# The one expert with two row blocks: its first layer's second half into the other four PSUM banks, and the next expert's first layer ahead of its second layer

## The chip, the cores and the metric

The kernel runs on one core of a Trainium2 chip. The metric is the device time of one execution in microseconds, taken as the median of several runs. The engines named below are TensorE (PE, matmuls; PEld is its weight load), VectorE (DVE), ScalarE (ACT), GpSimd (POOL) and SyncE (SP), which issues the weight loads.

## What is computed

One layer of a diffusion backbone over 512 latent tokens of width 1024: a state-space mixer with a pooling mixer, then a mixture of 32 experts of which each token takes four. The change lies in the mixture alone:

```python
def run_block(args):                 # hb: rows of tokens that chose expert e
    toks, e = args
    hb = x_pad[toks] @ w1[e] + b1[e]               # 1024 -> 2048: first layer
    g_part = jnp.minimum(hb[..., ::2], SWIGLU_LIMIT)
    u_part = jnp.clip(hb[..., 1::2], -SWIGLU_LIMIT, SWIGLU_LIMIT)
    act = g_part * jax.nn.sigmoid(SWIGLU_ALPHA * g_part) * (u_part + 1)
    return act @ w2[e] + b2[e]                     # 1024 -> 1024: second layer
```

The result of a row is multiplied by its gate and added to the token's row of the output. All is float32. An expert's weights are 12 MB, so the 32 experts read 384 MB.

## The kernel before

**Places and blocks.** Experts are taken in 32 places, sorted by how many tokens chose them. A place has a fixed number of rows: 64 (odd places here), or 80 to 128. Place 16 alone has two blocks, of 128 rows and of 64 rows, since the expert with the most tokens stands there.

**Pieces.** Weights come in pieces of 1 MB: `load` (line 1081, SP's queue) fills one of 11 `raw` tiles, and `split` makes of it a high part `hi` (ACT, line 1093) and a remainder `lo` (DVE, line 1094) that TensorE multiplies apart. There are three pairs of `hi` and `lo`, taken in turn. So a piece is split when TensorE is through with the piece three before it, and a load is issued when the `lo` of the piece eleven before it is made. A first layer is 8 pieces and a second layer 4; in place 16 the first layer is 4 pieces for its left half of columns (h = 0) and 4 for its right half (h = 1).

**Products.** `prod` (line 1357) multiplies one 128-deep slab of a piece into banks of 512 columns. A block with more than 64 rows takes three products for each bank (`hi` by `xh`, `hi` by `xl`, `lo` by `xh`). A block of 64 rows holds its own high and low parts side by side as 128 rows and takes two; its rows 64 to 127 are then added to its rows 0 to 63 by `rest` (ACT copies them to `b2h`, line 1326 or 1329) and a matmul with `slt`, beside the matmul that adds the bias (line 1337; for larger blocks line 1339).

**Banks.** PSUM has eight banks of 512 columns. Tag A is two tiles of two banks each (`bank("B")`), tag S four tiles of one bank (`bank("C")` for second layers, `bank("T")` for transposes). A first layer of an ordinary place fills the four banks of A. In place 16 each half fills them too: one tile for the 128-row block, one for the 64-row block. So h = 1 writes the banks out of which h = 0 is read.

**Activations.** `swiglu` reads a tile's columns (ACT line 1366; DVE lines 1371 and 1372), 1024 at a time, that is 512 gates and 512 values. `transposed` turns activations and gathered rows by TensorE (lines 1129 and 1139), ACT and DVE then making their high and low parts (lines 1131, 1132, 1143, 1144). `finish` (lines 1380 and 1382) scales a second layer's result and POOL adds it to the output rows in memory.

**Order.** In an ordinary place the second layer `C` of the place before is multiplied behind the first layer of the place, so that it covers the activations' work. Around place 16 the order of weights is: 16 left half with the second layer of 15 in its middle, 16 right half, then at once both blocks' second layer of 16 (bank S for block 0, bank A for block 1), then the first layer of 17. Nothing of another place stands between the right half and the second layer of 16. Within this, a scheduler sets the order of each engine's instructions when the program is built.

Of the kernel before, what the change touches and what calls it, by code (L numbers as in the profile page):

```python
# [97 lines left out]
def mixer_and_moe(tc, a):  # L98
# [1025 lines left out]
    def transposed(src, m, pool, name, bufs, tbank):  # L1124
        if m == LT:
            both = pool.tile([P, KT, 2, LT], F32R, name=name + "h", tag=name + "h", bufs=bufs)
            tp = tbank()
            for k in range(KT):
                PE.transpose(tp[:, k * LT:(k + 1) * LT], src[0:LT, k * P:(k + 1) * P], ident[0:LT, 0:LT])  # L1129
            v = tp.rearrange("p (k t) -> p k t", k=KT)  # L1130
            SC.activation(both[:, :, 0, :], v, AF.Copy)
            newest_part[0] = VE.tensor_tensor(both[:, :, 1, :], v, both[:, :, 0, :].bitcast(F32), op=ALU.subtract)  # L1132
            return (both.rearrange("p k i t -> p k (i t)"),)
        hi = pool.tile([P, KT, P], F32R, name=name + "h", tag=name + "h", bufs=bufs)
        lo = pool.tile([P, KT, P], F32R, name=name + "l", tag=name + "l", bufs=bufs)
        for h in range(2):
            tp = tbank()
            for k in range(4):
                PE.transpose(tp[:, k * P:k * P + m], src[0:m, (h * 4 + k) * P:(h * 4 + k + 1) * P],
                             ident[0:m, 0:m])  # L1140
            o = hi[:, h * 4:(h + 1) * 4, 0:m]
            v = tp.rearrange("p (k t) -> p k t", k=4)[:, :, 0:m]
            SC.activation(o, v, AF.Copy)
            newest_part[0] = VE.tensor_tensor(lo[:, h * 4:(h + 1) * 4, 0:m], v, o.bitcast(F32), op=ALU.subtract)  # L1144
        return hi, lo
# [112 lines left out]
def moe(tc, a, c_, cst, psa, psb, phx, pc, pd, g2, b1h, b2h, msum, top4, tab, last, table_out, acc_scr, halfneg,  # L1258
# [49 lines left out]
    def selector(p):  # L1308
        if CAPS[p][-1] == LT:
            SC.activation(slt[0:LT, 0:2, :], selm[0][0:LT, p:p + 1].unsqueeze(2).broadcast_to([LT, 2, LT]), AF.Copy)  # L1310
            SC.activation(slt[LT:P, 2, :], selm[0][LT:P, p:p + 1].broadcast_to([LT, LT]), AF.Copy)
            if len(CAPS[p]) == 1:
                return True
# [9 lines left out]
    def rest(banks):  # L1323

        if len(banks) == 1:
# [5 lines left out]
    def bias1(t, m, sl, h):  # L1331
        q = slice(2 * E * h, 2 * E * (h + 1))
        for j, bk in enumerate(halves(t)):
# [26 lines left out]
    def swiglu(t, m, out, plus=0.0):  # L1360

        v = t[0:m, :].rearrange("p (n two) -> p n two", two=2)
        n = 512
        g = pm.tile([P, n], F32, name="sg", bufs=SGB)[0:m, :]
        u = pm.tile([P, n], F32, name="su", bufs=SUB)[0:m, :]
# [32 lines left out]
    def C(p, blocks, sl=None, hooks=()):  # L1398
        e = ids[p]
        bks = [[bank("C") for _ in range(2)] if i == 0 else halves(bank("B")) for i in range(len(blocks))]  # L1400
# [11 lines left out]
        for (act, m, gcol, icol), bk in zip(blocks, bks):  # L1412
            if m == LT:
                rest(bk)
# [164 lines left out]
    for p in range(E):  # L1579
        e = ids[p] = expert(p)  # L1580
        m = CAPS[p][0]
        if p != MID:
# [23 lines left out]
            def first_half(h):  # L1606
                bias1(two[h], m, sl, h)
# [13 lines left out]
            else:  # L1621
                for h in range(2):
                    first_half(h)
                if pend is not None:
                    end = C(*pend)
            aT = transposed(act, m, "a", 1)
            pend = (p, [(aT, m, gtp[0][:, p:p + 1], ixi[0][:, p:p + 1])], sl)
        else:
# [3 lines left out]
            for h in range(2):  # L1632
                two = [bank("B") for _ in range(2)]
                for kk in range(KT // 2):
                    hi, lo = split(load(w1_pair(e, kk, h)))
                    for i in range(2):
                        q = slice(i * FF, (i + 1) * FF)
                        for j in range(2):
                            prod(halves(two[j]), ms[j], xs[j], 2 * kk + i, hi[:, q], lo[:, q])
# [3 lines left out]
                    if h == 0 and kk == 2:  # L1643
                        end()
                if h == 0:
                    sl = selector(p)
                rest([two[1]])
                for i in range(2):
                    bias1(two[i], ms[i], sl, h)
                    swiglu(two[i], ms[i], acts[i][:, h * 512:(h + 1) * 512])  # L1650
            aT0 = transposed(acts[0], ms[0], "a", 1)
            aT1 = transposed(acts[1], ms[1], "x", 1, (pc, phx)[nx[0] % 2])
            C(p, [(aT0, ms[0], gtp[0][:, p:p + 1], ixi[0][:, p:p + 1]), (aT1, ms[1], gt2[0], ix2[0][:, 0:1])], sl)()
            pend = end = None
            nxt = next_x(p + 1)
# [55 lines left out]
    if m == LT:  # L1711
        rest(bk)
# [110 lines left out]
```

## Time and profile before

| | before |
|---|---|
| median of 3 runs | 1787.97 us (1785.37 to 1789.52) |
| the profiled execution | 1785.24 us, of which its span is 1783.4 us |
| PE, DVE, ACT, POOL busy | 1634.9, 1524.0, 1170.2, 594.1 us |
| loads and stores of all queues | 521.44 MB, mean 292 GB/s |

The span runs from the first to the last instruction of the profiled execution; the execution's own time holds about 2 us more. The mixture of experts fills the last two thirds of the span, from about 640 us on. Busy times are averages over stages with different limits, so the rows below look at the stage around place 16 by itself.

### The profile page before, as it was taken

The numbers are of one execution on the slowest core, as the hardware profiler recorded it, in microseconds if no ns is written. First come the engines' busy times: TensorE is split into PE (matmuls) and PEld (weight loads), VectorE is DVE, ScalarE is ACT, GpSimd is POOL, SyncE is SP. The second block draws the span as 40 slices with busy tenths as digits, with TensorE's granted clock in tenths as the row PEclk, the third lists the DMA queues.
The fourth block names the chain that finished last, engine by engine and source line by source line (L and its number), as shares of the span: only waits on it lengthen the run. The fifth ranks groups of instructions, "written<-read, shape, count | busy, mean of one in ns | idle before, by whom it ended". The sixth has DMA issues, their size and how long they took to land. (4 is left out here: it accounts for less than half of the span.)

```text
span 1783.4 us, 21256 instructions
## 1 busy us (share of the span) xinstructions
PE 1634.9 (92%) x7311; PEld 1199.5 (67%) x7311; DVE 1524.0 (85%) x1486; ACT 1170.2 (66%) x1207; POOL 594.1 (33%) x287
## 2 busy tenths in 40 slices
PE   6999889998899899999999999999999998999995
PEld 2777667776777777767767667676666666666663
DVE  7767888987876989999989999966899999999994
ACT  6445336556643567787777877755678777787773
POOL 1213456779210102152040541502053454313302
PEclk9999899999999999999999999998999999999998
DMA  9646453323468789999999999985899999999973
GB/s 353 196 132 212 148 159 100 108 78 112 174 233 332 285 333 356 375 392 380 376 375 391 357 382 392 356 309 197 335 381 383 381 369 363 386 387 366 387 262 103
DMA packets 138417, 521.44 MB, mean 292 GB/s; under 512 B 14798, under 2 KB 44942, under 8 KB 106560
## 3 DMA queue, kind: packets, MB, share of 16 engines
q1 hardware_dynamic: 125446, 490.39, 72.4%
q0 software_dynamic: 6736, 16.70, 4.0%
q10 hardware_dynamic: 6122, 12.94, 2.2%
q8 instruction: 59, 0.97, 0.2%
q14 instruction: 54, 0.44, 0.1%
HBM read 508.26 MB, written 18.37 MB: 295 GB/s over the span
## 5 line engine op out<-in xcount | busy, mean ns | idle before, releaser
L1094 DVE TENSOR_TENSOR lo<-raw,hi 128x2048 fp32r<-128x2048 f32 x398 | 896.5, 2283 | 87.3 <-ACT hi L1093 83.3
L1093 ACT ACTIVATE hi<-raw 128x2048 fp32r<-128x2048 f32 x398 | 752.1, 1915 | 177.8 <-PE A L1357 111.0
L1382 POOL DMA_INDIRECT acc_scr<-y,ixi x32 | 216.7, 6773 | 544.8 <-DVE y L1380 444.6
L1357 PE MATMUL A<-lo,xh 128*128 128x512 f32 (+3 forms) x1072 | 315.4, 411 | 30.7 <-DVE lo L1094 26.7
L1357 PE MATMUL A<-hi,xh 128*128 128x512 f32 (+3 forms) x1072 | 308.9, 404 | 11.9 <-ACT hi L1093 8.0
L1357 PEld LDWEIGHTS A<-lo,xh 128*128 128x128 f32 (+3 forms) x1072 | 188.7, 185 | 117.7 <-DVE lo L1094 68.6
L1357 PEld LDWEIGHTS A<-hi,xh 128*128 128x128 f32 (+3 forms) x1072 | 194.7, 185 | 70.0 <-ACT hi L1093 10.6
L1117 POOL DMA_INDIRECT xg<-h_scr,ixi x30 | 113.1, 3771 | 256.5 <-PE S L1129 174.7
L1357 PE MATMUL S<-lo,ah 128*128 128x512 f32 (+3 forms) x512 | 163.9, 401 | 15.3 <-DVE lo L1094 15.2
L1357 PE MATMUL S<-hi,ah 128*128 128x512 f32 (+3 forms) x512 | 162.4, 398 | 1.7 <-DVE ah L1132 1.7
L1357 PE MATMUL A<-hi,xl 128*128 128x512 f32 (+3 forms) x544 | 154.5, 397 | 0.0
L1357 PEld LDWEIGHTS S<-lo,ah 128*128 128x128 f32 (+3 forms) x512 | 89.2, 181 | 50.3 <-DVE lo L1094 25.5
L1357 PEld LDWEIGHTS A<-hi,xl 128*128 128x128 f32 (+3 forms) x544 | 95.0, 175 | 31.7
L1357 PEld LDWEIGHTS S<-hi,ah 128*128 128x128 f32 (+3 forms) x512 | 91.1, 181 | 30.3 <-issue 3.1
L228 ACT ACTIVATE hi<-raw 128x1024 fp32r<-128x1024 f32 (+1 forms) x73 | 76.0, 1045 | 39.0 <-PE A L355 10.8
L231 DVE TENSOR_TENSOR lo<-raw,hi 128x1024 fp32r<-128x1024 f32 (+1 forms) x59 | 77.1, 1312 | 18.2 <-ACT hi L228 17.4
L1357 PE MATMUL S<-hi,al 128*128 128x512 f32 (+3 forms) x272 | 85.3, 394 | 0.0
L630 ACT ACTIVATE row<-row,nb 128x128 f32<-128x128 f32 x192 | 59.5, 389 | 37.1 <-POOL row L626 37.1
L336 PE MATMUL A<-hx,hi 128*128 128x512 f32 x160 | 66.2, 413 | 4.0 <-DVE at L378 2.5
L338 PE MATMUL A<-hx,lo 128*128 128x512 f32 x160 | 66.8, 417 | 0.0
L337 PE MATMUL A<-hx,hi 128*128 128x512 f32 x160 | 65.9, 412 | 0.0
L378 DVE SCALAR_TENSOR_TENSOR at<-A,cw,at 128x510 f32<-128x510 f32 (+1 forms) x80 | 57.8, 740 | 7.2 <-ACT at L374 6.6
(464 smaller groups left out, 2454.1 us busy)
## 6 DMA issues: line engine op xcount, KB each, us to landing
raw<-in_w_dram SPq DMA_DIRECT2D x384, 1024.0 KB
raw<-in_w_in_dram SPq DMA_DIRECT2D x36, 512.0 KB
mraw<-in_w_mod_dram SPq DMA_DIRECT2D x32, 512.0 KB
raw<-in_w_out_dram SPq DMA_DIRECT2D x14, 1024.0 KB
row<-cs_scr ACTq DMA_DIRECT2D x32, 384.0 KB
raw<-in_w_mod_dram SPq DMA_DIRECT2D x16, 512.0 KB
raw<-in_w_in_dram SPq DMA_DIRECT2D x16, 384.0 KB
xt<-in_x_dram SPq DMA_DIRECT2D x4, 512.0 KB
```

Of the source, the lines that this page charges most:

```text
L228: SC.activation(hi, r, AF.Copy)
L231: e.tensor_tensor(lo, r, hi.bitcast(F32), op=ALU.subtract)
L336: PE.matmul(lat, lhsT=hi[:, k, :], rhs=row_of(hxh, k), start=(k == 0), stop=False)
L337: PE.matmul(lat, lhsT=hi[:, k, :], rhs=row_of(hxl, k), start=False, stop=False)
L338: newest[0] = PE.matmul(lat, lhsT=lo[:, k, :], rhs=row_of(hxh, k), start=False, stop=(k == KT - 1))
L378: VE.scalar_tensor_tensor(ac[:, u:v], src[:, u + o:v + o], cw[:, j, ct:ct + 1], ac[:, u:v], op0=ALU.mult, op1=ALU.add)
L630: SC.activation(row[:, h, :], row[:, h, :], AF.Exp, bias=nb[:, c, i:i + 1])
L1093: ia = SC.activation(hi, r, AF.Copy)
L1094: i = VE.tensor_tensor(lo, r, hi.bitcast(F32), op=ALU.subtract)
L1117: PO.indirect_dma_start(out=t[0:m, :], out_offset=None, in_=h2_scr, in_offset=bass.IndirectOffsetOnAxis(ap=col[0:m, :], axis=0), bounds_ch ...
L1357: PE.matmul(bk[0:n, :], lhsT=u[:, k, 0:n], rhs=v[:, j * 512:(j + 1) * 512], start=(k == 0 and i == 0), stop=((last or m == LT and k == KT ...
L1382: PO.indirect_dma_start(out=acc_scr, out_offset=bass.IndirectOffsetOnAxis(ap=icol[0:m, :], axis=0), in_=y[0:m, :], in_offset=None, bounds_ ...
```

## The change

The right half of place 16 (h = 1) is written to the four banks of tag S, the left half stays in A. `swiglu` takes a bank at a time there (256 gates and 256 values) in both halves. The rows of place 17 are gathered and transposed inside the left half of 16, into a tile of their own (tag `xl` of pool phx, which a 64-row place doesn't use). The second layer of 16 is no longer done at the end of place 16 but is handed on as in the other places, so it stands behind the first layer of place 17; both its blocks use bank S, and its result is finished at once in place 17. For that, the part of `slt` which the second layer's bias takes is written in `rest`, just ahead of use, and no longer in `selector`: one instruction of 64 by 128 becomes two of 64 by 64, in all 64-row blocks.

```diff
     def selector(p):
         if CAPS[p][-1] == LT:
-            SC.activation(slt[0:LT, 0:2, :], selm[0][0:LT, p:p + 1].unsqueeze(2).broadcast_to([LT, 2, LT]), AF.Copy)
+            SC.activation(slt[0:LT, 0, :], selm[0][0:LT, p:p + 1].broadcast_to([LT, LT]), AF.Copy)
...
-    def rest(banks):
-
+    def rest(banks, p=None):
+
+
+        if p is not None:
+            SC.activation(slt[0:LT, B2, :], selm[0][0:LT, p:p + 1].broadcast_to([LT, LT]), AF.Copy)
...
     def swiglu(t, m, out, plus=0.0):
...
-        n = 512
-        g = pm.tile([P, n], F32, name="sg", bufs=SGB)[0:m, :]
-        u = pm.tile([P, n], F32, name="su", bufs=SUB)[0:m, :]
+        n = t.shape[-1] // 2
+        g = pm.tile([P, 512], F32, name="sg", bufs=SGB)[0:m, 0:n]
+        u = pm.tile([P, 512], F32, name="su", bufs=SUB)[0:m, 0:n]
...
     def C(p, blocks, sl=None, hooks=()):
         e = ids[p]
-        bks = [[bank("C") for _ in range(2)] if i == 0 else halves(bank("B")) for i in range(len(blocks))]
+        bks = [[bank("C") for _ in range(2)] for _ in blocks]
...
                 if pend is not None:
                     end = C(*pend)
+            if p == MID + 1:
+
+                end()
+                end = None
             aT = transposed(act, m, "a", 1)
...
             for h in range(2):
-                two = [bank("B") for _ in range(2)]
+
+                two = [[bank("C") for _ in range(2)] if h else halves(bank("B")) for _ in range(2)]
...
                     if h == 0 and kk == 2:
                         end()
+                        end = None
+
+                        nxt = transposed_(gather_(xgs[(nx[0] + 1) % 2], ixi[0][:, p + 1:p + 2], LT), LT,
+                                          (pc, phx)[nx[0] % 2], "x", 1, lambda: bank("T"), "xl")
                 if h == 0:
                     sl = selector(p)
-                rest([two[1]])
+                rest(two[1])
                 for i in range(2):
                     bias1(two[i], ms[i], sl, h)
-                    swiglu(two[i], ms[i], acts[i][:, h * 512:(h + 1) * 512])
+                    for j, bk in enumerate(two[i]):
+                        q = h * 512 + j * 256
+                        swiglu(bk, ms[i], acts[i][:, q:q + 256])
             aT0 = transposed(acts[0], ms[0], "a", 1)
             aT1 = transposed(acts[1], ms[1], "x", 1, (pc, phx)[nx[0] % 2])
-            C(p, [(aT0, ms[0], gtp[0][:, p:p + 1], ixi[0][:, p:p + 1]), (aT1, ms[1], gt2[0], ix2[0][:, 0:1])], sl)()
-            pend = end = None
-            nxt = next_x(p + 1)
+            pend = (p, [(aT0, ms[0], gtp[0][:, p:p + 1], ixi[0][:, p:p + 1]), (aT1, ms[1], gt2[0], ix2[0][:, 0:1])], sl)
```

Built programs show what this does to the order on an engine. First TensorE between the two halves of place 16, before. A is the tag of the banks, `sel` and `slt` rows are biases, `hi`, `xh` and the like rows are products.

```order
L1357 MATMUL A<-lo,xh 128x512 x2
L1339 MATMUL A<-b1h,sel 128x512 x2
L1337 MATMUL A<-b1h,slt 64x512
L1337 MATMUL A<-b2h,slt 64x512
L1337 MATMUL A<-b1h,slt 64x512
L1337 MATMUL A<-b2h,slt 64x512
L1357 MATMUL A<-hi,xh 128x512 x2
```

The same place in the change:

```order
L1360 MATMUL S<-lo,xh 128x512 x2
L1360 MATMUL S<-hi,xh 128x512 x2
L1340 MATMUL A<-b1h,slt 64x512
L1340 MATMUL A<-b2h,slt 64x512
L1340 MATMUL A<-b1h,slt 64x512
L1340 MATMUL A<-b2h,slt 64x512
L1360 MATMUL S<-hi,xl 128x512 x2
```

The 64-row block's biases, which stood ahead of the right half, now stand 22 products into it, and the right half's products go to S.

Next TensorE at the end of the right half, before; the rows with `con` are transposes of the activations, and `ah` and `al` their parts in the second layer of 16.

```order
L1357 MATMUL A<-lo,xh 128x512 x2
L1339 MATMUL A<-b1h,sel 128x512 x2
L1337 MATMUL A<-b1h,slt 64x512
L1337 MATMUL A<-b2h,slt 64x512
L1337 MATMUL A<-b1h,slt 64x512
L1337 MATMUL A<-b2h,slt 64x512
L1139 MATMUL S<-con_76,act 128x128 x4
L1129 MATMUL S<-con_76,act_9343 128x64 x4
L1357 MATMUL S<-hi,ah 128x512 x2
```

The same place in the change, where the A rows are the first layer of place 17:

```order
L1342 MATMUL S<-b1h,sel 128x512 x2
L1360 MATMUL A<-hi,xh 128x512 x4
L1360 MATMUL A<-lo,xh 128x512 x4
L1360 MATMUL A<-hi,xh 128x512 x4
L1360 MATMUL A<-lo,xh 128x512 x4
L1360 MATMUL A<-hi,xh 128x512 x4
L1340 MATMUL S<-b1h,slt 64x512
L1340 MATMUL S<-b2h,slt 64x512
L1340 MATMUL S<-b1h,slt 64x512
L1340 MATMUL S<-b2h,slt 64x512
L1360 MATMUL A<-lo,xh 128x512 x4
L1139 MATMUL S<-con_76,act 128x128 x4
```

Where the biases, the activations and their transposes stood one behind another, 20 products of place 17 now stand ahead of the biases, and four more ahead of the first transpose. Last, VectorE in the change while the first layer of 17 is multiplied; `su` and `act` rows are the activation's two steps, `al` and `xl` low parts behind transposes, `lo` the splits of pieces.

```order
L1094 TENSOR_TENSOR lo<-raw,hi 128x2048
L1375 SCALAR_TENSOR_TENSOR act<-sg,su 128x256
L1094 TENSOR_TENSOR lo<-raw,hi 128x2048 x2
L1374 TENSOR_SCALAR su<-S 64x256
L1144 TENSOR_TENSOR al<-S,ah 128x512
L1094 TENSOR_TENSOR lo<-raw,hi 128x2048
L1144 TENSOR_TENSOR al<-S,ah 128x512
L1375 SCALAR_TENSOR_TENSOR act_9349<-sg,su 64x256
L1094 TENSOR_TENSOR lo<-raw,hi 128x2048 x2
```

The activations of 16 are taken between the splits of place 17's pieces, where before they stood alone.

## Rows read from the trace of the kernel before

**Rows 1.** Page part 1: engine, busy us, share of span, instructions.

```profile
PE 1634.9 (92%) x7311; PEld 1199.5 (67%) x7311; DVE 1524.0 (85%) x1486; ACT 1170.2 (66%) x1207; POOL 594.1 (33%) x287
```

**Rows 2.** Windows: stretch, length, busy by engine, PEclk, DMA share, GB/s.

```profile
1130.00:1180.00 50.00, 49.64 (x218) 36.86 (x216) 44.45 (x29) 34.45 (x26) 17.72 (x4) 1.00 1.02 384
...
1180.00:1270.00 90.00, 80.82 (x326) 57.92 (x326) 55.04 (x43) 48.12 (x41) 11.64 (x5) 0.91 0.65 236
...
1270.00:1690.00 420.00, 398.92 (x1767) 275.43 (x1768) 393.79 (x263) 327.29 (x245) 158.18 (x23) 0.99 0.99 377
```

**Rows 3.** Windows of 10 us within that stage, same columns.

```profile
1190.00:1200.00 10.00, 10.00 (x45) 8.17 (x44) 6.39 (x4) 6.20 (x4) 0.00 (x0) 1.00 0.25 86
1200.00:1210.00 10.00, 7.42 (x26) 4.50 (x25) 6.72 (x7) 4.97 (x6) 0.00 (x0) 0.71 0.86 341
1210.00:1220.00 10.00, 10.00 (x48) 7.68 (x48) 0.69 (x1) 1.00 (x2) 0.16 (x1) 0.95 0.00 0
...
1230.00:1240.00 10.00, 7.88 (x28) 4.97 (x27) 6.12 (x8) 6.09 (x8) 3.51 (x1) 0.91 0.97 333
1240.00:1250.00 10.00, 9.85 (x37) 7.11 (x37) 9.99 (x5) 10.00 (x6) 3.21 (x1) 0.92 0.90 277
```

**Rows 4.** Waits of SP's queue, 1040 to 1330 us: total, times, longest.

```profile
SPq L1081 <- DVE lo L1094: 241.1, 88, 19.2
```

**Rows 5.** Timeline of DVE: start, us, operation, [idle before <-releaser].

```profile
1183.73 2.29 DVE L1094 TENSOR_TENSOR lo<-raw,hi 128x2048 fp32r<-128x2048 f32 x1 [0.39 <-ACT hi L1093]
...
1194.20 6.88 DVE L1094 TENSOR_TENSOR lo<-raw,hi 128x2048 fp32r<-128x2048 f32 x3 [2.94 <-ACT hi L1093]
1203.41 2.29 DVE L1094 TENSOR_TENSOR lo<-raw,hi 128x2048 fp32r<-128x2048 f32 x1 [2.33 <-ACT hi L1093]
...
1223.13 6.69 DVE L1094 TENSOR_TENSOR lo<-raw,hi 128x2048 fp32r<-128x2048 f32 x3 [2.21 <-ACT hi L1093]
...
1240.01 17.71 DVE L1094 TENSOR_TENSOR lo<-raw,hi 128x2048 fp32r<-128x2048 f32 x8 [2.29 <-ACT hi L1093]
...
1268.73 6.69 DVE L1094 TENSOR_TENSOR lo<-raw,hi 128x2048 fp32r<-128x2048 f32 x3 [1.51 <-ACT hi L1093]
```

**Rows 6.** Timeline of PE, same columns.

```profile
1180.09 0.73 PE L1339 MATMUL A<-b1h,sel 64*128 64x512 f32 x2
1183.24 0.63 PE L1357 MATMUL A<-hi,xl 128*128 128x512 f32 x2
1183.71 0.63 PE L1357 MATMUL A<-lo,xh 128*128 128x512 f32 x2
...
1204.47 0.69 PE L1337 MATMUL A<-b1h,slt 128*64 128x512 f32 x1 [1.93 <-ACT b2h L1326]
...
1207.09 1.11 PE L1139 MATMUL S<-con,act 128*128 128x128 f32 x4 [0.65 <-DVE act L1372]
...
1254.21 0.45 PE L1337 MATMUL A<-b1h,slt 128*64 128x512 f32 x1 [1.84 <-ACT b2h L1326]
...
1257.06 0.69 PE L1337 MATMUL A<-b1h,slt 128*64 128x512 f32 x1 [1.72 <-ACT b2h L1326]
...
1269.90 0.71 PE L1129 MATMUL S<-con,xg 64*128 64x64 f32 x8
```

**Rows 7.** Groups by shape, 1153 to 1290 us: busy, mean ns, idle before.

```profile
L1094 DVE TENSOR_TENSOR lo<-raw,hi 128x2048 fp32r<-128x2048 f32 x35 | 78.7, 2287 | 15.5 <-ACT hi L1093 15.4
...
L1144 DVE TENSOR_TENSOR al<-S,ah 128x512 fp32r<-128x512 f32 x2 | 1.4, 692 | 3.6 <-ACT ah L1143 3.6
...
L1144 DVE TENSOR_TENSOR xl<-S,xh 128x448 fp32r<-128x448 f32 x2 | 1.2, 608 | 0.0
...
L1311 ACT ACTIVATE slt<-selm 64x64 fp32r<-64x64 f32 x2 | 0.5, 252 | 2.6 <-PE A L1337 2.6
```

**Rows 8.** Timeline of POOL: the gather of place 17's 64 rows.

```profile
1126.43 13.67 POOL L1117 DMA_INDIRECT xg<-h_scr,ixi  x1 [0.31 <-PE A L1357]
```

More of the change, by code (lines that the diff above doesn't have):

```diff
@@ L1122, in mixer_and_moe, with transposed @@
     newest_part = [None]
-    def transposed(src, m, pool, name, bufs, tbank):
+    def transposed(src, m, pool, name, bufs, tbank, tag=None):
         if m == LT:
-            both = pool.tile([P, KT, 2, LT], F32R, name=name + "h", tag=name + "h", bufs=bufs)
+            both = pool.tile([P, KT, 2, LT], F32R, name=name + "h", tag=tag or name + "h", bufs=bufs)
             tp = tbank()
@@ L1329, in rest, with bias1 @@
                 SC.activation(b2h[LT:P, j * 512:(j + 1) * 512], bk[LT:P, :], AF.Copy)
-    def bias1(t, m, sl, h):
+    def bias1(bks, m, sl, h):
         q = slice(2 * E * h, 2 * E * (h + 1))
-        for j, bk in enumerate(halves(t)):
+        for j, bk in enumerate(bks):
             js = slice(j * 512, (j + 1) * 512)
@@ L1413, in C @@
             if m == LT:
-                rest(bk)
+                rest(bk, p)
         def end():
@@ L1606, in first_half @@
             def first_half(h):
-                bias1(two[h], m, sl, h)
+                bias1(halves(two[h]), m, sl, h)
                 swiglu(two[h], m, act[:, h * 512:(h + 1) * 512])
@@ L1638, in moe @@
                         for j in range(2):
-                            prod(halves(two[j]), ms[j], xs[j], 2 * kk + i, hi[:, q], lo[:, q])
+                            prod(two[j], ms[j], xs[j], 2 * kk + i, hi[:, q], lo[:, q])
                     if h == 0 and kk == 1:
@@ L1711, in moe @@
     if m == LT:
-        rest(bk)
+        rest(bk, p)
     x = bias2(bk, m, sl)
```

## The prediction

> **What bounds the kernel now.** I read the page's busy table first: no engine is full, TensorE at 92% and VectorE at 85% come nearest [rows 1], so the limit must be sought by stage. Windows of the mixture come next. On either side of place 16 the DMA engines have no spare time: a share of 1.02 at 384 GB/s in the 50 us before, 0.99 at 377 GB/s in the 420 us behind [rows 2]. There the weight loads bound the kernel, at 1.049 MB / 0.38 MB per us = 2.76 us for a piece. From 1180 to 1270 us their share is 0.65, that is 0.35 x 90 = 31.5 us in which nothing was loaded [rows 2]. This is the kernel's visible loss in the mixture, and the change works in just this stage.
>
> Why the loads stop is seen in three views. SP's queue waits for one thing alone, the making of `lo` by DVE (88 waits, the longest 19.2 us) [rows 4]: a load goes out when the split eleven pieces back is done. DVE's splits have a hole from 1186.0 to 1194.2, since the right half of 16 has to go tile by tile, and one from 1205.7 to 1223.1, and few of them until 1240 [rows 5]; the loads' share is 0.25 in 1190 to 1200 and 0.00 in 1210 to 1220 [rows 3]. The splits in turn wait for ACT's `hi`, which waits for TensorE to free one of the three pairs. So in this stage TensorE's progress bounds the loads. It is a heavy place: 16 has 16 slabs of 10 products in its first layer and 8 of 10 in its second, and one product takes (1183.71 - 1183.24) / 2 = 0.235 us [rows 6]; a piece of two slabs and 20 products takes 4.7 us, against 2.76 us for its load. But TensorE also wastes time: it is busy 80.8 of 90 us, so idle 9.2, and the granted clock is 0.91 of full, 0.09 x 90 = 8.1 us more [rows 2]. Together 17.3 us. The waits are those of the tail of 16: 1.93 us for `b2h` and 0.65 us for the activations near 1205, 1.84 and 1.72 us at the end of place 17 [rows 6], and behind each pair of them the clock falls to its lower level of 1.2 GHz for a few microseconds (shares of 0.71, 0.91 and 0.92) [rows 3].
>
> **The change, part by part.** I count from TensorE's first bias of the left half, 1180.09, to the transposes at 1269.90 which in the program stand behind three slabs of place 18: 89.8 us before [rows 6]. The same work in the new order:
>
> 1. Bias of the 128-row block 0.73 us [rows 6], and the 64-row block's four biases, now inside the right half, 4 x 0.235 = 0.9. The right half follows at once, since the banks of S are free. 80 products: 18.8 us. One wait between the halves goes (the copy to `b2h` and the activations no longer stand ahead of it).
> 2. Bias in S, 0.7. Place 17's first layer, 64 products or 15.0 us on TensorE, but DVE paces it. Two of its eight pieces are split before the right half ends, since three pairs are in turn; six remain, 6 x 2.287 = 13.7 us [rows 7]. DVE also takes the activations of 16 there: four pieces of two operations, 256 wide. From 512 columns at 692 ns and 448 at 608 ns, a column costs 1.3 ns [rows 7], so 256 take about 692 - 256 x 1.3 = 0.36 us, and eight 2.9. Two low parts behind transposes take 1.4, two more (place 18's rows) 1.2. Sum 19.2 us, with a piece's latency 20. The transposes and the 64-row block's biases fit into TensorE's 5 us of slack there.
> 3. At the end of 17 the copy to `b2h` is still waited for, once, 1.84 us; its second wait of 1.72 is covered, since 16 products of the second layer of 16 now stand between. Eight biases: 1.9.
> 4. Second layer of 16: 80 products, 18.8 us, bias 0.7, last transposes 0.3. Then three slabs of place 18, 36 products, 8.5 us. Four banks of A are free by then, so they go at full pace.
> 5. Place 17's transposes, moved into the left half: 0.7 us, taken by 1180 us.
>
> Sum 0.7 + 0.9 + 18.8 + 0.7 + 20 + 1.8 + 1.9 + 18.8 + 1.0 + 8.5 + 0.7 = 73.8 us, against 89.8: 16.0 us less. That is near the 17.3 us that TensorE wastes now, as it should be. I take off one fall of the clock, of the smallest size seen, (0.09 + 0.08) x 10 = 1.7 us [rows 3], for the wait at the end of 17: 14.3 us.
>
> The loads must gain as much for it to count. They lose 31.5 us now. In the new order they still lose in the right half, 4 x (4.7 - 2.76) = 7.8 us, and in the second layer of 16. There TensorE takes block 0 for three pieces before it touches block 1, so no pair comes free for the 36 products of block 0, the eight biases, the wait and the first eight products of block 1, about 8.5 + 1.9 + 1.8 + 1.9 = 14 us; a few loads stand out at its start, so perhaps 9 us are lost. 31.5 - 16.8 = 14.7 us, in agreement. Behind 18 the two kernels are alike, and as the loads are full for 420 us there (0.99) [rows 2], what they gain should last to the end.
>
> Edits at no cost: place 17's gather runs at 1126.43 in the old program already, 13.67 us on POOL [rows 8], because the scheduler took it ahead, and its place in POOL's queue is the same; its rows are there 20 us before they are wanted. Were they late, TensorE would stand in the middle of the left half, at most for the gather's 13.67 us. The split of `selector` adds one instruction of 0.25 us [rows 7] in each 64-row place, 16 or so, 4 us in all on ACT, which is busy 66% [rows 1]; loads hide it, and without that cover it would cost 4 us. At the last place, 0.25 us may show. ACT's activations by halves add eight fixed costs at the most, likewise below 2 us, between its splits. The new waits on TensorE's queue are for `b2h` at the start of the right half and for the copies from S during 17; behind them stand products whose operands are ready, so what they hold up is counted above as slack of 5 us.
>
> TensorE's clock is the term I trust least. In the rows it falls after waits of about 2 us on a lightly fed TensorE, 3.4 us lost near 1205 ((0.29 + 0.05) x 10) [rows 3]. The Trainium skill (TensorE: Matmul & The Clock Gate, section "A second HAM failure mode: psum-queue depth-cycling") says that a TensorE which idles briefly and often between groups of products can swing between its two clock levels, and loses throughput although each product is fast. By that rule a first layer paced by DVE, as place 17's becomes, would swing, and the gain would be that of the first rival below, 7.5 us, not 14.3. The trace bears it out in place 17 before; in the 50 us from 1130 on, where most of place 15's first layer is multiplied at a like pace, it doesn't (granted clock 1.00) [rows 2].
>
> **Rivals.**
> - *The clock falls three times, as now.* Place 17 is fed by DVE with gaps, and two waits remain. For it: 1.72 and 1.84 us of wait did it at 17 before [rows 6]. Against it: 16 products now part the waits. Price: two more falls of 3.4 us, gain 14.3 - 6.8 = 7.5 us: by the sum below, 1779.
> - *The loss only moves.* The second layer of 16 stands behind 17 and holds all three pairs; if the pieces loaded by then are too few, places 18 to 20 wait for data, and the hole of 14 us comes back in full with the 7.8 us of the right half, and the catching up of 17 at DVE's pace is lost too (20 - 15 = 5 us): 31.5 - 14 - 7.8 - 5 = 4.7 us, and with one more fall 1.3: no difference, about 1786.
> - *Slower: the clock stays low.* If TensorE, once it has fallen at the start of 17, doesn't rise until the second layer of 16 is through, the 15.0 + 18.8 us of products take twice that, of which 5 are slack of 17: 28.8 us lost, 14.5 slower, 1802. It decides once more than 14.3 us of full-clock products run at the lower level. Against it: the fall near 1205 was over soon in 1210 to 1220 (0.95), on dense products [rows 3].
> - *All of the loss goes.* If the loads keep up (more of them outstanding, no wait at the second layer of 16), up to 24 us may be won; 1764.
>
> **How the numbers follow.** Chances: forecast 0.57 (gain 9 to 20 us), three falls 0.19, loss only moves 0.10, slower 0.08, more than forecast 0.06. The sum is made against the profiled execution, 1785.2 us, and gives 1785.2 - 14.3 = 1770.9; the median of the runs shown is 2.8 us higher, which gives 1773.7. I say 1772. About 0.2% (3.6 us) is what a measurement of this kernel can tell from no change. The range 1764 to 1784 holds the forecast, the three falls and all but the extreme of "all goes"; outside stand most of "only moves" and the slower case. Faster by more than that: 0.57 + 0.19 + 0.06 = 0.82; within it 0.10; slower 0.08.
>
> **What would show it.** In the profile after: TensorE's products to S begin within 1 us of the bias at the left half's end; no wait for `act` at 0.65 us and no wait of 1.93 for `b2h` at the end of the right half; place 17's first layer takes about 20 us with DVE nearly full; the loads' share shows a dip in the right half and one of about 9 us in the second layer of 16, and no window of 0.00; the transposes that stood at 1269.90 come near 1254 to 1256; the lower clock appears once between 1200 and 1245. It would be wrong if TensorE waits for VectorE in place 17 for more than 5 us, if the clock stays at its lower level through the second layer of 16, or if loads behind 1270 are below a share of 0.97, so that time won is lost again.

## The result and the profile after

| | before | after |
|---|---|---|
| median, four runs each | 1787.68 us (1785.37 to 1789.52) | 1768.12 us (1763.72 to 1769.41) |
| the profiled execution, its span | 1785.24, 1783.4 us | 1769.41, 1767.6 us |

The ratio is 0.9898, 95% interval 0.9883 to 0.9913: the change makes the kernel faster, by 19.6 us between the medians and by 18.2 us from the ratio. The two profiled executions are 15.8 us apart, for that of before is shorter than any of these four runs and that of after is the longest. Line numbers are those of each run's own kernel: `prod` is L1357 before and L1360 after.

The busy times of the page, against [rows 1], tell nearly nothing:

```profile
PE 1626.3 (92%) x7311; PEld 1197.6 (68%) x7311; DVE 1524.6 (86%) x1494; ACT 1170.6 (66%) x1229; POOL 551.7 (31%) x287
```

The stages do. Windows after, columns as in [rows 2]:

```profile
1130.00:1180.00 50.00, 49.71 (x225) 37.10 (x224) 44.43 (x29) 36.41 (x28) 18.66 (x4) 1.00 1.02 379
1180.00:1270.00 90.00, 89.01 (x402) 67.13 (x401) 72.31 (x59) 60.97 (x56) 20.77 (x5) 1.00 0.86 303
1270.00:1410.00 140.00, 132.62 (x590) 92.56 (x589) 130.36 (x89) 108.39 (x85) 36.01 (x8) 1.00 0.99 380
```

In the stage around place 16 TensorE is busy 89.0 of 90 us, against 80.8, its granted clock is 1.00, against 0.91, and the loads' share is 0.86, against 0.65 [rows 2]. Ahead of it the rows are alike. For what follows, the third of these windows in the kernel before:

```profile
1270.00:1410.00 140.00, 133.28 (x595) 92.98 (x596) 132.17 (x89) 110.67 (x84) 60.61 (x9) 1.00 0.98 375
```

Windows of 10 us after, which answer to [rows 3]:

```profile
1190.00:1200.00 10.00, 10.00 (x45) 8.09 (x44) 6.71 (x9) 4.10 (x3) 0.00 (x0) 1.00 0.69 238
1200.00:1210.00 10.00, 10.00 (x46) 7.44 (x45) 7.51 (x8) 8.05 (x8) 0.00 (x0) 1.00 0.67 245
1210.00:1220.00 10.00, 10.00 (x53) 7.91 (x52) 10.00 (x9) 9.93 (x11) 0.00 (x0) 1.00 0.95 348
1220.00:1230.00 10.00, 9.01 (x40) 6.48 (x39) 9.96 (x10) 6.66 (x9) 9.48 (x1) 1.00 0.91 334
1230.00:1240.00 10.00, 10.00 (x45) 7.87 (x45) 5.62 (x6) 5.72 (x4) 0.00 (x0) 1.00 0.60 206
1240.00:1250.00 10.00, 10.00 (x43) 7.32 (x42) 8.03 (x7) 6.31 (x6) 0.62 (x1) 1.00 0.94 335
```

No window from 1180 to 1270 us is empty of loads any more, and none has a lower clock. The shares of 0.69 and 0.67 are the right half of 16, the 0.60 is its second layer. TensorE's timeline after, against [rows 6]:

```profile
1181.92 0.73 PE L1342 MATMUL A<-b1h,sel 64*128 64x512 f32 x2
1182.58 0.73 PE L1360 MATMUL S<-hi,xh 128*128 128x512 f32 x2
...
1202.26 0.73 PE L1342 MATMUL S<-b1h,sel 64*128 64x512 f32 x2
1202.92 1.19 PE L1360 MATMUL A<-hi,xh 128*128 128x512 f32 x4
...
1220.79 1.20 PE L1360 MATMUL A<-lo,xh 128*128 128x512 f32 x4 [0.35 <-DVE lo L1094]
...
1222.63 0.45 PE L1340 MATMUL A<-b1h,slt 128*64 128x512 f32 x1 [0.64 <-ACT b2h L1329]
...
1223.62 0.40 PE L1360 MATMUL S<-hi,ah 128*128 128x512 f32 x1
...
1233.30 0.63 PE L1360 MATMUL S<-hi,xh 128*128 128x512 f32 x2
...
1253.93 0.66 PE L1129 MATMUL S<-con,xg 64*128 64x64 f32 x8
```

The right half starts in S 0.66 us behind the bias, the first layer of 17 starts 0.66 us behind the right half's bias, and the only waits of any size are 0.35 us for a `lo` and 0.64 us for `b2h`. From the bias to the transposes that stood at 1269.90 it is 1253.93 - 1181.92 = 72.0 us, against 89.8. The stretch starts 1.8 us later than before, for place 17's transposes stand ahead of it now and this execution was already 1.3 us behind at the gather (1127.72 against 1126.43 [rows 8]); it ends 1269.90 - 1253.93 = 16.0 us earlier. SP's longest wait for `lo` (1040 to 1330 us) falls from 19.2 [rows 4] to 9.4 us:

```profile
SPq L1081 <- DVE lo L1094: 214.9, 87, 9.4
```

### The profile page after: what moved, and what is told of

Same layout as the page of the kernel before. It is cut to its first block, busy times and chain, and to the rows that moved or that the text cites. A ratio compares the mean times of both kernels' runs of the same rounds, so it can differ in the third digit from the quotient of the medians.

```text
span 1767.6 us, 21305 instructions
## 1 busy us (share of the span) xinstructions
PE 1626.3 (92%) x7311; PEld 1197.6 (68%) x7311; DVE 1524.6 (86%) x1494; ACT 1170.6 (66%) x1229; POOL 551.7 (31%) x287
## 4 chain that ended last, share of the span: by engine, by line
PE 49%; DVE 17%; DMA 14%; issue 10%; ACT 4%; POOL 4%; SPq 0%; DVEq 0%; POOLq 0%; ACTq 0%
PE A L1360 21%; PE S L1360 12%; DVE lo L1094 8%; DMA raw<-in_w_dram 5%; DMA acc_scr<-y,ixi 3%; ACT hi L1093 2%; DMA mraw<-in_w_mod_dram 2%; PE A L736 1%; PE A L737 1%; PE A L740 1%; PE A L1340 1%; DVE ac L459 1%; PE A L353 1%; PE A L354 1%; DMA raw<-in_w_mod_dram 1%
## 5 line engine op out<-in xcount | busy, mean ns | idle before, releaser
L1360 PE MATMUL A<-lo,xh 128*128 128x512 f32 (+3 forms) x1024 | 297.1, 410 | 30.0 <-DVE lo L1094 25.9
L1385 POOL DMA_INDIRECT acc_scr<-y,ixi x32 | 161.2, 5038 | 505.6 <-DVE y L1383 383.9
L1360 PE MATMUL A<-hi,xh 128*128 128x512 f32 (+3 forms) x1024 | 290.4, 403 | 11.2 <-ACT hi L1093 8.6
L1360 PEld LDWEIGHTS A<-lo,xh 128*128 128x128 f32 (+3 forms) x1024 | 179.1, 184 | 114.1 <-DVE lo L1094 67.6
L1117 POOL DMA_INDIRECT xg<-h_scr,ixi x30 | 128.0, 4267 | 323.3 <-PE S L1129 157.3
L1360 PEld LDWEIGHTS A<-hi,xh 128*128 128x128 f32 (+3 forms) x1024 | 184.4, 184 | 65.4 <-ACT hi L1093 11.4
L1360 PE MATMUL S<-lo,ah 128*128 128x512 f32 (+3 forms) x512 | 164.2, 401 | 14.8 <-DVE lo L1094 14.7
L1360 PE MATMUL S<-hi,ah 128*128 128x512 f32 (+3 forms) x512 | 161.8, 396 | 1.6 <-DVE ah L1132 1.6
L1360 PE MATMUL A<-hi,xl 128*128 128x512 f32 (+3 forms) x528 | 147.6, 396 | 0.0
L1360 PEld LDWEIGHTS S<-lo,ah 128*128 128x128 f32 (+3 forms) x512 | 88.9, 180 | 48.4 <-DVE lo L1094 23.6
L1360 PEld LDWEIGHTS A<-hi,xl 128*128 128x128 f32 (+3 forms) x528 | 91.8, 174 | 30.9
L1360 PEld LDWEIGHTS S<-hi,ah 128*128 128x128 f32 (+3 forms) x512 | 91.0, 180 | 30.9 <-issue 3.9
L231 DVE TENSOR_TENSOR lo<-raw,hi 128x1024 fp32r<-128x1024 f32 (+1 forms) x59 | 77.0, 1310 | 19.6 <-ACT hi L228 18.6
L1360 PE MATMUL S<-hi,al 128*128 128x512 f32 (+3 forms) x272 | 85.3, 393 | 0.0
```

Of the source, the lines that this page charges most:

```text
L231: e.tensor_tensor(lo, r, hi.bitcast(F32), op=ALU.subtract)
L1117: PO.indirect_dma_start(out=t[0:m, :], out_offset=None, in_=h2_scr, in_offset=bass.IndirectOffsetOnAxis(ap=col[0:m, :], axis=0), bounds_ch ...
L1360: PE.matmul(bk[0:n, :], lhsT=u[:, k, 0:n], rhs=v[:, j * 512:(j + 1) * 512], start=(k == 0 and i == 0), stop=((last or m == LT and k == KT ...
L1385: PO.indirect_dma_start(out=acc_scr, out_offset=bass.IndirectOffsetOnAxis(ap=icol[0:m, :], axis=0), in_=y[0:m, :], in_offset=None, bounds_ ...
```

## Experiments

The table gives every run beside the kernel before on the same chip. "TensorE lost" is worked out for 1180 to 1270 us as in the prediction: 90 us less its busy time, and 90 us times what its clock lacks. "Loads lost" is the share that the DMA engines lacked there and in 1270 to 1410 us, times the lengths. "Less" is (1 - ratio) x 1787 us. Shares are rounded to hundredths, so that a loss is good to about 1 us. The ratio and "less" are from all executions of a run, the two columns of losses from its profiled one alone; that of e1_banks is its slowest, 1797.25 us.

| run | ratio to before (95%) | less, us | TensorE lost | loads lost |
|---|---|---|---|---|
| before | 1 | 0 | 9.2 + 8.1 = 17.3 | 31.5 + 2.8 = 34.3 |
| after | 0.9898 (0.9883 to 0.9913) | 18.2 | 1.0 + 0 = 1.0 | 12.6 + 1.4 = 14.0 |
| e1_banks | 0.9985 (0.9972 to 0.9998) | 2.7 | 8.7 + 8.1 = 16.8 | 24.3 + 7.0 = 31.3 |
| e2_order | 0.9971 (0.9957 to 0.9985) | 5.2 | 8.0 + 5.4 = 13.4 | 27.9 + 0 = 27.9 |
| e3_rows | 1.0032 (1.0022 to 1.0043) | -5.7 | 14.2 + 8.1 = 22.3 | 31.5 + 7.0 = 38.5 |
| e4_small | 1.0028 (1.0012 to 1.0043) | -5.0 | 13.8 + 9.9 = 23.7 | 31.5 + 7.0 = 38.5 |
| e5_fill | 0.9983 (0.9970 to 0.9996) | 3.0 | 8.0 + 0 = 8.0 | 28.8 + 2.8 = 31.6 |
| e6_rows_act | 1.0010 (0.9998 to 1.0023) | -1.8 | 12.5 + 7.2 = 19.7 | 31.5 + 4.2 = 35.7 |
| e7_order_act | 0.9954 (0.9937 to 0.9971) | 8.2 | 6.7 + 1.8 = 8.5 | 23.4 + 1.4 = 24.8 |
| e8_less | 0.9887 (0.9867 to 0.9906) | 20.2 | 1.1 + 0 = 1.1 | 8.1 + 4.2 = 12.3 |
| e9_b1first | 0.9933 (0.9913 to 0.9952) | 12.0 | 3.0 + 5.4 = 8.4 | 18.9 + 1.4 = 20.3 |
| e10_inter0 | 0.9935 (0.9919 to 0.9951) | 11.6 | 3.0 + 3.6 = 6.6 | 19.8 + 1.4 = 21.2 |
| e10_inter1 | 0.9918 (0.9901 to 0.9936) | 14.7 | 1.3 + 0 = 1.3 | 14.4 + 1.4 = 15.8 |

In all of these the loading that was lost less agrees with the time that was won, within 4 us and mostly within 2. TensorE's lost time says the same within about 3 us except where its work differs: e5_fill has 6.3 us of work more, e8_less 7.5 us less.

**The parts by themselves.** First the banks and the small edits alone, the second layer of 16 at once as before. From the changed kernel:

```diff
-            pend = (p, [(aT0, ...), (aT1, ...)], sl)
+            C(p, [(aT0, ...), (aT1, ...)], sl)()
+            pend = end = None
+            nxt = next_x(p + 1)
...
```

> The right half of place 16 in the banks of tag S and its activations bank by bank, but the second layer of 16 done at once as before, and place 17's rows gathered behind it. Theory (the time was lost in the waits of TensorE at the tails of 16 and 17 and in the clock that falls behind them, and the new order is what covers them): only the 1.2 us between the halves go, 1783 to 1787. Rival (the loads' hole while the right half goes tile by tile out of A was the loss, so the banks are what counts): 8 us less or more, 1780 or below.

Median 1783.78 us. The theory holds, the rival falls. The right half no longer waits, but the tails do (`b2h` 1.54 us and activations 0.83 us at the end of the right half, `b2h` 1.84 and 1.75 us at the end of 17), and the clock falls as before, so that the TensorE time lost in the stage stays at 16.8 us.

Then the order alone: second layer of 16 behind 17's first layer, both halves in A, activations 512 wide.

```diff
-                two = [[bank("C") for _ in range(2)] if h else halves(bank("B")) for _ in range(2)]
+                tt = [bank("B") for _ in range(2)]
+                two = [halves(t) for t in tt]
...
```

> The new order alone: both halves of place 16 in the banks of tag A with activations 512 wide, place 17's rows early and its first layer ahead of the second layer of 16. Theory: most of the gain, but place 17 waits until the right half's banks are read, 2 to 4 us with a fall of the clock, so 1770 to 1777. Rival (the banks are what counts): within 5 us of the kernel before, 1783 to 1788.

Median 1781.21 us: 4 us above the theory's bound. TensorE's timeline at the start of the right half, first in the kernel before:

```profile
1182.67 0.74 PE L1357 MATMUL A<-hi,xh 128*128 128x512 f32 x2 [0.20 <-DVE su L1371]
```

The same place in e2_order, and the end of its right half:

```profile
1188.55 1.22 PE L1360 MATMUL A<-hi,xh 128*128 128x512 f32 x2 [3.72 <-DVE su L1374]
...
1211.55 0.45 PE L1340 MATMUL A<-b1h,slt 128*64 128x512 f32 x1 [1.45 <-ACT b2h L1329]
```

The right half waits 3.72 us for the activations to free A, where it waited 0.20 us before, and the clock is lower behind it (0.92 and 0.91 in the two windows from 1180 to 1200 us). To see which edit brought that, the early rows of place 17 alone, put into the kernel before:

```diff
                     if h == 0 and kk == 2:
                         end()
+                        end = None
+                        nxt = transposed_(gather_(xgs[(nx[0] + 1) % 2], ixi[0][:, p + 1:p + 2], LT), LT,
+                                          (pc, phx)[nx[0] % 2], "x", 1, lambda: bank("T"), "xl")
...
-            nxt = next_x(p + 1)
```

> The kernel before with place 17's rows gathered and transposed inside the left half of place 16, nothing else. Theory: 0.7 us of transposes move out of the stage that TensorE bounds, so 0 to 1 us less, no difference that can be measured. Rival (the early rows let place 17 start earlier): 3 us or more.

Median 1791.15 us, slower by 0.32%, which neither expected. The start of its right half, from the timelines; ScalarE first:

```profile
1182.35 1.91 ACT L1093 ACTIVATE hi<-raw 128x2048 fp32r<-128x2048 f32 x1
1184.29 1.07 ACT L1366 ACTIVATE sg<-A 128x512 f32<-128x512 f32 x2
```

VectorE there:

```profile
1184.30 2.29 DVE L1094 TENSOR_TENSOR lo<-raw,hi 128x2048 fp32r<-128x2048 f32 x1 [2.76 <-ACT hi L1093]
1186.51 0.68 DVE L1371 TENSOR_SCALAR su<-A 128x512 f32<-128x512 f32 x1
```

TensorE, the first products of the right half:

```profile
1187.25 1.22 PE L1357 MATMUL A<-hi,xh 128*128 128x512 f32 x2 [3.72 <-DVE su L1371]
```

And ScalarE in the kernel before:

```profile
1181.30 0.60 ACT L1366 ACTIVATE sg<-A 128x512 f32<-128x512 f32 x1
1181.79 1.91 ACT L1093 ACTIVATE hi<-raw 128x2048 fp32r<-128x2048 f32 x1
```

Before, `sg` of the first tile stands ahead of the next piece's `hi`. With the early rows the built program has the `hi` (1.91 us) ahead of `sg` on ScalarE, and the `lo` (2.29 us) ahead of `su` on VectorE. The bank is freed by `su`, so the products behind it wait 3.72 us, and the granted clock is 0.73 in the window from 1180 to 1190 us. The Trainium skill (PSUM — Partial Sum Buffer, section "Engine vs sequencer instructions") says that ScalarE's and VectorE's queues are strictly first in, first out; the trace agrees, with `sg` at 1184.29 just behind a `hi` that the waiting products didn't need.

The small edits alone (one instruction for the selector into two, 256-wide activations) do the like:

```diff
...
-                    swiglu(two[i], ms[i], acts[i][:, h * 512:(h + 1) * 512])
+                    for j, bk in enumerate(halves(two[i])):
+                        q = h * 512 + j * 256
+                        swiglu(bk, ms[i], acts[i][:, q:q + 256])
...
```

> The kernel before with the split of the selector instruction in all 64-row places and the activations of place 16 by 256 columns, nothing else. Theory: hidden by loads, within 1 us of the kernel before. Rival (each of 16 instructions of 0.25 us on ACT counts): 4 us slower, 1791 to 1792.

Median 1791.74 us. The rival's time came, but the profile puts the loss elsewhere than it said. TensorE loses 6.4 us more than before in the stage around place 16 (23.7 against 17.3), which is more than the whole 5.0, and there is a wait of 3.20 us, for the second bank's `sg` stands behind a `hi` on ScalarE. The two edits weren't run apart. ScalarE's timeline, then TensorE's:

```profile
1180.72 0.39 ACT L1368 ACTIVATE sg<-A 128x256 f32<-128x256 f32 x1
1181.01 1.91 ACT L1093 ACTIVATE hi<-raw 128x2048 fp32r<-128x2048 f32 x1
1182.81 0.38 ACT L1368 ACTIVATE sg<-A 128x256 f32<-128x256 f32 x1
```

The products that wait for it:

```profile
1185.72 1.19 PE L1359 MATMUL A<-hi,xh 128*128 128x512 f32 x2 [3.20 <-DVE su L1373]
```

Two kernels then mend VectorE's order by a rule: the `lo` of the right half's third piece behind the left half's first activation. In e6 it is added to the early rows alone, in e7 to the order alone.

```diff
                     hi, lo = split(load(w1_pair(e, kk, h)))
+                    if h == 1 and kk == 2:
+                        after(newest_lo[0], first_act, "the activations go ahead")
...
```

> The early rows alone as in the kernel that was measured 4 us slower than before, with one more rule of order: VectorE's split of the third piece of the right half stands behind the first activation of the left half, not ahead of it. Theory (that kernel lost its time because VectorE split a piece ahead of the activation that frees bank A, TensorE standing 3.7 us at the start of the right half, with a fall of the clock): the wait returns to 0.2 us and the time to that of before, 1785 to 1788. Rival (the gather or the transposes of the early rows cost the time): 1790 to 1792 as without the rule.

> The new order alone, both halves in the banks of tag A, with the same rule of order for VectorE. Theory: the 3.7 us at the start of the right half and the fall of the clock behind it go, so 5 us less than without the rule, 1774 to 1778; what is left against the whole change are the waits between the right half and place 17. Rival (the new order alone is worth little, the banks as such are needed): 1780 to 1782 as without the rule.

Medians 1788.28 and 1777.99 us. e7's time is within its theory's range, e6's 0.3 us above it. Against e3 the ratio of e6 is lower clear of the noise, so it was in the main the order that the early rows cost, and neither the gather nor the transposes. The wait falls to 2.14 us in either, not to 0.2, since the rule holds VectorE's `lo` alone and ScalarE's `hi` still stands ahead of `sg`. Of e7:

```profile
1186.82 0.74 PE L1360 MATMUL A<-hi,xh 128*128 128x512 f32 x2 [2.14 <-DVE su L1374]
...
1208.68 0.45 PE L1340 MATMUL A<-b1h,slt 128*64 128x512 f32 x1 [1.92 <-ACT b2h L1329]
```

So the order has 1.6 us less of wait and 3.6 us less of lost clock, and e7's ratio is 3.0 us below e2's; the two intervals overlap, so the 3 us aren't clear of the noise.

**The clock by itself.** Products that nobody reads, 26 in all, fill the tails of 16 and 17 in the kernel before.

```diff
+    def fill(n, u, v):
+        t = bank("T")
+        for _ in range(n):
+            PE.matmul(t, lhsT=u[:, 0, 0:P], rhs=v[:, 0:512], start=True, stop=True)
...
+                if p == MID + 1:
+                    fill(8, x[0], lo)
...
+                else:
+                    fill(10, xs[1][0], lo)
```

> The kernel before with products that nothing reads (10 at the end of the right half of 16, 16 at the end of place 17, 0.235 us each) set where TensorE waits for the copies to b2h. Theory (the clock falls because TensorE waits there): the lower clock near 1205 and 1255 goes, 6.8 us of it at each place, so 3.4 us each are won, less 0.4 and 1.9 us by which the fillers outlast the waits: 3 to 5 us less, 1782 to 1785. Rival (the clock falls there for another reason, or costs nothing since loads bound the stage): the lower clock stays, and 0 to 2 us more, 1787 to 1790.

Its window over the stage:

```profile
1180.00:1270.00 90.00, 81.97 (x362) 59.95 (x361) 56.05 (x44) 46.53 (x40) 12.41 (x5) 1.00 0.68 247
```

The fillers as a group by shape: count, busy, mean ns, idle before.

```profile
L1425 PE MATMUL S<-lo,xh 128*128 128x512 f32 x26 | 6.3, 392 | 0.0
```

Median 1783.68 us: the theory's time holds, and its rival falls. The granted clock is 1.00 in the whole stage, against 0.91. It isn't one execution alone: over the whole span the clock was 0.975 to 0.978 in ten executions, against 0.966 to 0.976 in 19 of the kernel before. So the fillers hold the clock up. That a wait by itself brings it down isn't shown: waits of 2.08 us for the activations, of 1.72 us for `b2h`, and of 0.92 and 1.20 us in 17's first layer are left in this profile, and no fall stands behind any of them. The 8.1 us of clock come back less 6.3 us for the fillers; waits shrink by 1.2 us. That leaves 17.3 - 8.0 - 6.3 = 3.0 us, which is what was measured. The loads still lose 28.8 us in the stage: a clock held up by work that isn't wanted is worth little here.

**What bounds the changed kernel in the stage.** 32 of the 64-row block's products are left out of the right half and the second layer of 16, 7.5 us of TensorE: those of its rows with the weights' `lo`.

> The changed kernel with part of the computation left out: in the right half and the second layer of place 16 the 64-row block takes one product in place of two for each bank (32 products, 7.5 us of TensorE). Loads are the same. Theory (after the change the stage is bound by TensorE's products alone, loads waiting for them): 6 to 8 us less than the changed kernel, 1760 to 1762. Rival (loads or VectorE bound the stage now): within 2 us of the changed kernel, 1766 to 1769.

Its windows over the stage and behind it:

```profile
1180.00:1270.00 90.00, 88.89 (x394) 65.43 (x393) 77.11 (x62) 66.17 (x61) 17.28 (x5) 1.00 0.91 331
1270.00:1410.00 140.00, 129.82 (x576) 89.92 (x575) 127.35 (x87) 105.42 (x82) 62.58 (x8) 1.00 0.97 366
```

Median 1767.4 us: the same as the changed kernel. The theory falls and the rival's time holds: in the changed kernel TensorE's products in this stage aren't what sets the time. In the stage the loads lose 4.5 us less than after (0.91 against 0.86), but 2.8 us more in the 140 us behind it (0.97 against 0.99). Why they are lost there, and what sets the time instead, was not settled; from 1330 to 1370 us TensorE waits 5.4 us in all for `lo` in it, against 3.9 us after.

The dip of 0.60 in 1230 to 1240 us was taken up next. VectorE in that stretch of the changed kernel:

```profile
1236.83 4.49 DVE L1094 TENSOR_TENSOR lo<-raw,hi 128x2048 fp32r<-128x2048 f32 x2 [4.06 <-ACT hi L1093]
```

It idles 4.06 us for `hi`, that is for a free pair, as the prediction described for the second layer of 16. Two kernels let TensorE take both blocks piece by piece, by holding back the `lo` of the second layer's first piece (inter0) or second piece (inter1).

```diff
             hi, lo = split(load(w2_pair(e, kk)))
+            if p == MID and kk == 0:
+                after(newest_lo[0], part1, "both blocks go together")
```

> The changed kernel with one rule more in the second layer of place 16: VectorE's low part of its first piece stands behind block 1's transposed activations, so that TensorE takes both blocks piece by piece there and the three pairs come free one after another, not all behind 36 products of block 0. Theory (the loads' dip of 1230 to 1240, share 0.60, comes from the three held pairs, and loads that aren't lost there count to the end): 2 to 5 us below the changed kernel, 1763 to 1766, with a share above 0.8 in each 10 us of the second layer. Rival (as with the products left out, loads gained around place 16 are given back by place 21, since the stretch behind is bound by something else too): 1767 to 1770, the same as the changed kernel. Second rival (the split that waits stands ahead of place 17's work on VectorE's queue, and TensorE waits for it): 1772 to 1780, with a wait for the low part of 2 us or more near 1225.

> As the run with the rule at the first piece, but the rule at the second piece: block 0's first piece goes ahead, then both blocks together. It holds VectorE's queue less, and frees the first pair no earlier than the changed kernel. Theory (held pairs cost loads): 1 to 3 us below the changed kernel, 1765 to 1767. Rival (given back): 1767 to 1770. Second rival (a split that waits): 1770 to 1776.

Medians 1772.01 and 1769.45 us. The theory falls with both; in inter1 the first rival's time (given back) holds, and its interval overlaps that of the changed kernel. In inter1 the dip moves, from 1230 to 1240 into 1240 to 1250 us, and isn't gone:

```profile
1230.00:1240.00 10.00, 10.00 (x46) 8.12 (x44) 5.89 (x3) 3.89 (x3) 0.00 (x0) 1.00 0.82 285
1240.00:1250.00 10.00, 10.00 (x45) 6.70 (x44) 8.65 (x8) 7.58 (x7) 3.50 (x1) 1.00 0.67 223
```

From 1220 to 1260 us the loads lose 6.0 us in it and 5.9 us in the changed kernel: the order in which the pairs come free didn't change the sum. That fits an estimate: 80 products take 18.8 us and the layer's four loads 4 x 2.76 = 11.0, so about 7.8 us have to be lost in either order. In inter0 the second rival's time holds, though the wait is for `b2h` and not for the low part:

```profile
1226.64 0.69 PE L1340 MATMUL A<-b1h,slt 128*64 128x512 f32 x1 [2.61 <-ACT b2h L1329]
```

Last, the right half's tail with the 64-row block ahead of the 128-row block:

```diff
-                for i in range(2):
+                for i in ((1, 0) if h else (0, 1)):
```

> The changed kernel with the biases and activations of the right half taken for the 64-row block ahead of the 128-row block. Theory (nothing waits for the order of the two there, since place 17's first layer covers both): within 2 us of the changed kernel, 1766 to 1770. Rival (what comes first on ScalarE and VectorE moves a split, as in the runs where early rows alone cost 3 us): 1771 to 1775, with a wait of 2 us or more between 1202 and 1225.

TensorE at the end of 17's first layer in it:

```profile
1221.04 0.45 PE L1340 MATMUL A<-b1h,slt 128*64 128x512 f32 x1 [0.64 <-ACT b2h L1329]
...
1224.16 0.69 PE L1340 MATMUL A<-b1h,slt 128*64 128x512 f32 x1 [1.99 <-ACT b2h L1329]
```

Its windows of 10 us there:

```profile
1220.00:1230.00 10.00, 7.37 (x31) 4.57 (x30) 9.64 (x11) 8.90 (x12) 0.43 (x1) 0.68 1.00 381
1230.00:1240.00 10.00, 10.00 (x37) 8.05 (x37) 3.79 (x7) 2.59 (x3) 0.55 (x1) 0.81 0.52 166
```

Median 1773.23 us: the rival holds, with a wait of 1.99 us and a clock fall of (0.32 + 0.19) x 10 = 5.1 us behind it. The products of 16's second layer, which stand between the two groups of biases in the changed kernel, come behind both here. That is the first rival of the prediction in small: with a second wait at 17's end and one fall back, 18.2 - 12.0 = 6.2 us of the gain go, for the order of two blocks.

## Why the prediction was right

**What bounds the stage: right for the kernel before.** The 17.3 us that TensorE wasted were named as what there is to win; 1.0 is left of them, and the loads' loss fell from 31.5 to 12.6 us. Across the runs above, these two track the time. For the changed kernel it holds no longer: 7.5 us less of TensorE's work bought 2.0 us by the ratios, within the noise (e8_less).

**The sum: right in the whole, with terms off both ways.** Bias and right half with four biases took 1202.26 - 1181.92 = 20.3 us (20.4 forecast). 17's first layer took 19.1 us up to the wait for `b2h` (20). That wait was 0.64 us (1.84). The second layer of 16, three slabs of 18 and the last four biases took 1253.93 - 1223.62 = 30.3 us (28.3 + 0.9 = 29.2). With the 0.7 us of transposes that the prediction counts ahead of the stretch, 72.7 us stand against its 73.8, or against 75.5 with the clock's 1.7.

VectorE was at work without a gap from 1203.85 us to the end of 17's first layer, as said. But TensorE was busy 18.7 of 19.1 us there too:

```profile
1202.92:1221.99 19.07, 18.72 (x91) 14.40 (x90) 18.00 (x15) 18.52 (x20) 1.54 (x1) 1.00 0.85 311
```

64 products, four biases and the transposes of 16 and of the next rows leave little of the 5 us of slack that had been reckoned. Which of the two engines set the layer's length this run can't tell, so that 20 us came near is in part luck. The 256-wide operation is 0.42 us, not 0.36:

```profile
L1375 DVE SCALAR_TENSOR_TENSOR act<-sg,su 128x256 f32<-128x256 f32 x4 | 1.7, 423 | 0.1
```

**The clock: the term that failed.** One fall of 1.7 us was taken off the 16.0; there was none. With TensorE filled there, waits of 0.35 and 0.64 us left it at 1.00. The rows were misread as well. The prediction puts the shares of 0.91 and 0.92 [rows 3] behind the waits of 1.84 and 1.72 us at the end of 17, but those windows end at 1250 us and the waits at 1254 and 1257. The fall of 1.7 us stands inside 17's first layer, behind two shorter waits (products of 0.43 us in place of 0.235), in the kernel before:

```profile
1235.39 0.73 PE L1357 MATMUL A<-lo,xh 128*128 128x512 f32 x2 [0.92 <-DVE lo L1094]
1237.33 0.70 PE L1357 MATMUL A<-hi,xh 128*128 128x512 f32 x2 [1.20 <-DVE y L1380]
...
1238.40 1.06 PE L1357 MATMUL A<-hi,xh 128*128 128x512 f32 x2
```

The end of 17 has a fall of its own there, of (0.23 + 0.11) x 10 = 3.4 us:

```profile
1250.00:1260.00 10.00, 6.38 (x20) 3.65 (x19) 9.30 (x7) 6.30 (x7) 0.00 (x0) 0.77 1.01 402
1260.00:1270.00 10.00, 10.00 (x43) 6.89 (x42) 3.01 (x4) 3.81 (x3) 0.00 (x0) 0.89 0.54 220
```

By this row the forecast would have been 16.0 - 3.4 = 12.6 us. The Trainium skill (TensorE: Matmul & The Clock Gate, section "A second HAM failure mode: psum-queue depth-cycling"), which the prediction weighed, says that short and frequent idling between groups of products made the clock of one kernel swing. In 17's first layer after, TensorE hardly idled, so the case didn't arise. For the layer as it was before, the runs disagree: the same waits of 0.92 and 1.20 us have a fall behind them in the kernel before and in e1_banks (0.83 in 1240 to 1250 us), and none in e4_small and e5_fill (1.00). Place 15's first layer, which the prediction sets against the rule, runs from 1116.5 to 1138.2 us, so that less than half of it lies in the window that it names; the clock was 1.00 in all of it, with waits of 1.38 and 1.29 us.

**The gain kept to the end: right.** The stretch ends 16.0 us earlier and the profiled execution is 15.8 us shorter; behind 1270 the loads lose 1.4 us, before 2.8. The loss in the right half (0.69 and 0.67, 6.4 us against 7.8 expected) and the one in the second layer of 16 (5.5 us in the three windows from 1220 us on, against about 9 expected) are where they were put. The second is smaller: from the end of the wait to block 1's first product it is 1233.30 - 1222.63 = 10.7 us, where 8.5 + 1.9 + 1.8 had been reckoned with the wait, but that is 1.5 us only, and where the rest lies wasn't taken apart.

**Edits at no cost: right in the whole, wrong apart.** The gather came early as said and hid:

```profile
1127.72 13.66 POOL L1117 DMA_INDIRECT xg<-h_scr,ixi  x1 [0.30 <-PE A L1360]
```

The early rows and the small edits were priced by their own instructions. By themselves they cost 5.7 and 5.0 us, by what they do to the built order: a split ahead of the activation that frees A. In the change this doesn't show, as the right half doesn't wait for A. The parts don't add up: 2.7 us for the banks and 5.2 for the order, or 8.2 with its rule, make 7.9 to 10.9, and together they are worth 18.2. Either alone keeps waits that the whole change doesn't have (e1_banks those of the tails, e7_order_act 2.14 and 1.92 us), with 8.1 and 1.8 us of lost clock. That this is all of the difference is argued, not shown.

**The size.** 14.3 us were forecast against the profiled execution, which gave 15.8, and the median went from 1787.7 to 1768.1 where 1772 was said. By the prediction's own sum it would be 1773.7; it says 1772 without a reason, and so came 1.7 us nearer by luck. Of the 5.6 us from 1773.7, 2.8 are in the stretch, in the main 1.7 for the clock, 1.2 for the wait for `b2h` and 0.9 for 17's first layer, less 1.1 that the last part took longer. The rest is within what the runs of one kernel differ by.

## What to carry to other kernels

Where a stage is bound by loads on either side, count the loading that is lost in it (share lacking times length) and what the pacing engine wastes there by waits and clock: in these runs both gave the time within a few microseconds, while busy times over the whole span said nothing. Cost an edit by the place that it gets in every in-order queue, not only by its own duration: edits priced at nothing cost 5 us by themselves. Parts of a change that each leave one wait in the same chain must be tried together.

## What was not expected of the hardware

Behind waits of the same length the clock fell in one kernel's profile and not in another's. The right half starts behind a wait of 2.14 us in both e6_rows_act and e7_order_act; the windows there, in this order:

```profile
1180.00:1190.00 10.00, 7.35 (x24) 4.81 (x23) 5.95 (x6) 4.00 (x4) 2.39 (x1) 0.83 0.79 283
...
1180.00:1190.00 10.00, 7.35 (x31) 4.90 (x30) 6.58 (x6) 4.15 (x5) 3.21 (x1) 1.00 0.90 333
```

The pair of 0.92 and 1.20 us in 17's first layer did so too, as told above. In e5_fill a wait of 2.08 us left the clock at 1.00; in e9_b1first waits of 0.64 and 1.99 us, with 1.1 us of biases between them, brought it down to 0.68 and 0.81 in two windows. So the length of a wait alone doesn't decide whether the clock falls; what does, these runs don't settle. Whether a fall that one profile shows stands in other executions of the same kernel isn't shown either, for each was profiled once; a forecast that prices it from one row should say so.
